# HGRN2 layer on one core: a head's normalised output is kept in z, and its transposes and stores are issued after the next head's projections

## The chip, the cores and the metric

The kernel runs on one NeuronCore of a Trainium2 chip. The metric is the device time of one execution in microseconds; three runs of the kernel before took 3592.83, 3593.45 and 3589.02 us, median 3592.83. The engines of the core are named as in the profile: PE (TensorE, matrix products; PEld is its weight load), DVE (VectorE), ACT (ScalarE), POOL (GpSimd) and SP (SyncE, which only issues transfers here). Each engine works through its own instructions in order, and waits for others by semaphores.

## The reference

Two layers over 1024 latent tokens and 256 context tokens of width 1024. The first runs neighbourhood attention and a bidirectional mLSTM side by side; the second, the one that the change touches, is a bidirectional HGRN2 with 16 heads of key and value width 128. Its essentials (cut):

```python
def project(h):
    q, f_fwd, f_bwd, i, z = _split_cols(h @ w_in, C_SIZES)
    def decay(f_pre):
        f = lb + (1.0 - lb) * jax.nn.sigmoid(f_pre.astype(F32))
        return _bht(_heads(1.0 - f, HG_HEADS)), _bht(_heads(jnp.log(f), HG_HEADS))
    rec = (_bht(_heads(jax.nn.silu(q), HG_HEADS)), _bht(_heads(i, HG_HEADS)), (decay(f_fwd), decay(f_bwd)))
    return rec, z

o_l, o_c = _gla_bidir(rec_l, rec_c, need_ctx)   # gated linear attention, forward plus backward in time

def merge(o, z):
    o = _rms(jnp.swapaxes(o, 1, 2).astype(z.dtype), h_norm.reshape(HG_HEADS, HG_VDIM))
    return (o.reshape(o.shape[:2] + (HG_VW,)) * jax.nn.silu(z)) @ w_out
```

For each head, then: o is computed for all 1024 latent tokens, divided by its root mean square over the 128 channels, scaled per channel by `h_norm`, and multiplied by silu(z). The products of all heads go through `w_out`.

## The kernel before

The kernel is written in a tile framework. The program states operations in a sequence with tiles from pools; a scheduler then orders the instructions on each engine, by priority (the place in the program) and by a time model of its own, and sets the semaphores. A tile of a tag with `bufs` n waits until the tile n places before it in the same tag has been released by all who write or read it.

All large products are made of float32 operands that are split in a high and a low part (`split`, L69 to L72, the high part by ACT, the low one by DVE), in three matmuls for each slab of 128 rows (L117 to L119, and L729 to L731 in the output projection). Their results stand in the PSUM tag `mm`, which has two banks.

The HGRN2 layer runs head by head (L170 to L177), and the scheduler interleaves neighbouring heads:

- `hg_proj` (L756) computes the two decays F (L769, L770) and the query q = silu (L778, L779; `gq`) transposed, with the tokens along the free axis: matmuls of 256 or 512 columns.
- `hg_intra` (L838) and `hg_level` (L884) work out the products within blocks of 128 tokens in seven levels: copies `gksel` by ACT (L893), products by PE (L898), masks and decays by DVE (L905, L907, L918, L920). `hg_near` (L925 to L936) treats neighbours, and `hg_close` (L858) the diagonal; its low part shares the tag `gyt`, one buffer, with the output's eviction.
- `hg_vz` (L782) projects v and z in natural layout, tokens on partitions, two token tiles at a time into one bank of 2 x 256 columns. ACT copies v out (L801), takes the sigmoid of z (L803) and copies z out (L804); POOL multiplies the two in place (L805). The tile z (`gz`) has one buffer for all heads. A first product for the context is copied to `gEc` and transposed (L794).
- `hg_ctx` (L809) makes the states that come out of the context, with scans on DVE (L817, L818) that are started by two memsets (L814, L815).
- `hg_scan` (L938) goes over the eight blocks of 128 tokens. In each, three products (L958, L959, L960) add up in one quarter of the PSUM bank `acc` (one bank); a product of keys and values (L963) and a step on DVE (L965) carry the state on. After four blocks, half a head, the end is worked off:

```python
for i in range(4):
    nc.scalar.activation(jk, o4[:, i, :], AF.Square, accum_out=ss[:, i : i + 1])        # L974, ACT
self.rsqrt(ss, ss, 1.0 / P)                                                             # L142, L144, POOL
pt = self.ps("tr", [P, 4, P])
for i in range(4):
    yn = self.t(pool, [P, P], F32, "gyn", 2)                                            # ring of two
    nc.vector.scalar_tensor_tensor(                                                     # L979, DVE
        out=yn, in0=o4[:, i, :], scalar=ss[:, i : i + 1], in1=z[:, c - 3 + i, :], op0=ALU.mult, op1=ALU.mult)
    nc.tensor.transpose(pt[:, i, :], yn, self.ident)                                    # L982, PE
yt = self.t(pool, [P, 512], F32, "gyt", 1)
nc.scalar.activation(yt, ..., AF.Copy, scale=self.hnc[:, h : h + 1])                    # L984, ACT
nc.gpsimd.dma_start(out=y[h, :, ...], in_=yt)                                           # L985, POOL queue
```

So half a head is four products of 128 x 128 on DVE, four transposes on PE, one eviction of 128 x 512 on ACT and one store to the scratch tensor `yd2` in DRAM.

After the last head, the output projection reads `yd2` back (L716), splits it (`out_y`, L710) and multiplies it by w_out (`out_sum`, L723). For the columns 512 to 1023 it is done in two parts: heads 0 to 7 for all eight token tiles (L1184 to L1187), which the scheduler interleaves with head 15, and then heads 8 to 15 (`out_tile`, L734). The token tiles 0 to 3 need the first half of head 15 from `yd2`, the tiles 4 to 7 the second. SP issues these loads in one queue with the loads of the weights (L97).

Of the kernel before, what the change touches and what calls it, by code (L numbers as in the profile page):

```python
# [9 lines left out]
F32 = mybir.dt.float32  # L10
# [3 lines left out]
ALU = mybir.AluOpType  # L14
# [4 lines left out]
P = 128  # L19
# [24 lines left out]
class Prog:  # L44
# [890 lines left out]
        nc.vector.tensor_tensor(out=pr[1], in0=pr[1], in1=q, op=ALU.mult)  # L935
        H["near"] = pr  # L936

    def hg_scan(self, h, st, halves, S, pool, y):  # L938
        nc = self.nc
        v, z = st["v"], st["z"]  # L940
        Sf, Sb = S
        sb = {7: Sb}
        for c in range(7, 0, -1):
            H = halves[c // 4]
            u = self.ps("s", [P, P])
            nc.tensor.matmul(u, lhsT=H["kn"][1][:, c % 4, :], rhs=v[:, c, :], start=True, stop=True)
            s = self.t(pool, [P, P], F32, "gS1", 10)
            nc.vector.scalar_tensor_tensor(
                out=s, in0=sb[c], scalar=H["T"][:, 1, c % 4 : c % 4 + 1], in1=u, op0=ALU.mult, op1=ALU.add
            )  # L950
            sb[c - 1] = s
        for c in range(8):
            H = halves[c // 4]
            cs = slice((c % 4) * P, (c % 4 + 1) * P)
            if c % 4 == 0:
                o4 = self.ps("acc", [P, 4, P])
            o = o4[:, c % 4, :]
            nc.tensor.matmul(o, lhsT=H["A"][:, c % 4, :], rhs=v[:, c, :], start=True, stop=False)  # L958
            nc.tensor.matmul(o, lhsT=H["Q"][:, 0, cs], rhs=sb[c], start=False, stop=False)  # L959
            nc.tensor.matmul(o, lhsT=H["Q"][:, 1, cs], rhs=Sf, start=False, stop=True)  # L960
            if c < 7:
                u = self.ps("s", [P, P])
                nc.tensor.matmul(u, lhsT=H["kn"][0][:, c % 4, :], rhs=v[:, c, :], start=True, stop=True)  # L963
                s = self.t(pool, [P, P], F32, "gS0", 2)
                nc.vector.scalar_tensor_tensor(  # L965
                    out=s, in0=Sf, scalar=H["T"][:, 0, c % 4 : c % 4 + 1], in1=u, op0=ALU.mult, op1=ALU.add
                )
                Sf = s
            if c % 4 < 3:
                continue  # L970
            ss = self.t(pool, [P, 4], F32, "gss", 2)
            jk = self.t(pool, [P, P], F32, "gjk", 1)
            for i in range(4):
                nc.scalar.activation(jk, o4[:, i, :], AF.Square, accum_out=ss[:, i : i + 1])  # L974
            self.rsqrt(ss, ss, 1.0 / P)
            pt = self.ps("tr", [P, 4, P])
            for i in range(4):
                yn = self.t(pool, [P, P], F32, "gyn", 2)
                nc.vector.scalar_tensor_tensor(  # L979
                    out=yn, in0=o4[:, i, :], scalar=ss[:, i : i + 1], in1=z[:, c - 3 + i, :], op0=ALU.mult, op1=ALU.mult  # L980
                )
                nc.tensor.transpose(pt[:, i, :], yn, self.ident)  # L982
            yt = self.t(pool, [P, 512], F32, "gyt", 1)
            nc.scalar.activation(yt, pt.rearrange("p a b -> p (a b)"), AF.Copy, scale=self.hnc[:, h : h + 1])  # L984
            nc.gpsimd.dma_start(out=y[h, :, (c // 4) * 512 : (c // 4 + 1) * 512], in_=yt)  # L985


    def build(self):
        tc, nc, a = self.tc, self.nc, self.a
        dma = nc.sync.dma_start  # L990
        with ExitStack() as es:
# [19 lines left out]
            def load(name, shape, eng=nc.gpsimd):  # L1011
# [12 lines left out]
                out=self.qkn, in0=qkn[:, 0:1], scalar1=qkn[:, 1:2], scalar2=0.125, op0=ALU.mult, op1=ALU.mult  # L1024
# [14 lines left out]
            for i in range(2):  # L1039
# [6 lines left out]
                out=self.lb[:, 1, :], in0=self.lb[:, 0, :], scalar1=-1.0, scalar2=1.0, op0=ALU.mult, op1=ALU.add  # L1046
# [31 lines left out]
            with tc.tile_pool(name="na", bufs=2) as pool, self.pp.phase(tq=1, s=2, acc=1):  # L1078
                qk = self.na_qk(0, pool)
                z = self.na_z(0, pool)  # L1080
                ahead = [("o", 0), ("z", 0), ("o", 1), ("z", 1), ("o", 2), ("z", 2), ("q", 0), ("k", 0)]
                for p2 in range(8):
# [7 lines left out]
                    if p2 < 7:  # L1090
                        z = self.na_z(p2 + 1, pool)
# [30 lines left out]
            with tc.tile_pool(name="op0", bufs=2) as op, ExitStack() as wl:  # L1122
# [3 lines left out]
                for tt in [8, 9, 3, 4, 2, 5, 1, 6, 0, 7]:  # L1126
# [14 lines left out]
                    out=self.ones, in0=self.ident, scalar1=0.0, scalar2=1.0, op0=ALU.mult, op1=ALU.add  # L1141
# [23 lines left out]
            with l1:  # L1165
                pool = l1.enter_context(tc.tile_pool(name="hg", bufs=2))
                self.rawp = pool
                l1.enter_context(self.pp.phase(s=3, acc=1))
                st = self.hg_proj(0, pool, wf)
                for h in range(16):  # L1170
                    hv = self.hg_intra(st, pool)
                    self.hg_vz(h, st, pool)
                    self.hg_close(hv, pool)
                    S = self.hg_ctx(st, pool)
                    self.hg_scan(h, st, hv, S, pool, self.yd2)
                    if h < 15:
                        st = self.hg_proj(h + 1, pool)

                right.close()
                yp = es.enter_context(tc.tile_pool(name="oy", bufs=1, side="right"))  # L1180
                acc = self.t(yp, [P, 8, 512], F32, "oacc", 1)
                rows = lambda q, b: a["woc"][q * D : (q + 1) * D, b * 512 : (b + 1) * 512]
                w = self.wblock(yp, "wo", [rows(0, 1)], 8, 512, yp, 4, "woraw", ring=8)
                for tt in range(8):  # L1184
                    ps = self.ps("mm", [P, 512])
                    self.out_sum(ps, w, tt, (0,), self.yd2, yp, 2)
                    nc.scalar.copy(acc[:, tt, :], ps)  # L1187
                w2 = self.wblock(yp, "wo", [rows(1, 1)], 8, 512, yp, 4, "woraw", ring=8)
# [152 lines left out]
```

## Time and profile before

| | us |
|---|---|
| median of three runs | 3592.83 |
| lowest, highest | 3589.02, 3593.45 |
| the profiled execution | 3587.84 |
| its span in the profile | 3586.1 |
| PE busy in the span | 3495.6 |
| DVE, ACT, POOL busy | 2235.0, 1456.0, 527.6 |
| mean granted clock of PE (full speed is 1) | 0.992 |

The profile shows one execution. Its page gives busy times by engine, the granted clock in 40 slices, the transfers, and the costliest groups of instructions by source line. Other views of the trace give the waits of one engine (who waited for whom, us in total, times, longest), the busy time by stretch, and the instructions in order of time. In the latter a row has the start, the duration in us, engine, line, operation, the tiles (output <- inputs), shapes and how many were merged; in square brackets stands the idle time of the engine just before, and what ended it. Ends of matmuls are modelled, since they are pipelined: two neighbouring ones overlap, and the distance of their starts says what one costs. In a row of the busy time by stretch stand the stretch, its length, then the busy time and the number of instructions of PE, PEld, DVE, ACT and POOL, the granted clock, the share of the transfer engines' time, and GB/s. The layer takes about 92 us a head, from 1900 to 3450 us of the span.

### The profile page before, as it was taken

What the parts mean: (1) busy time and instruction counts of PE and PEld (TensorE: products, weight loads), DVE (VectorE), ACT (ScalarE), POOL (GpSimd) and SP (SyncE); (2) the same over time, 40 slices, a digit from 0 to 9 for tenths busy, and PEclk for the clock granted to TensorE, in tenths of its full rate; (3) what the DMA queues carried; (4) which work ended last, traced back from release to release, by engine and by line L of the source; (5) the groups of instructions that cost most, each with busy time, mean ns of one, the idle gap of its engine ahead of it and who ended that gap; (6) DMA issues with size and microseconds to landing.
All of it is one profiled execution on the core that took longest, in us unless ns stands there. A gap on an engine that the chain in (4) does not pass through costs nothing.

```text
span 3586.1 us, 64157 instructions
## 1 busy us (share of the span) xinstructions
PE 3495.6 (97%) x24570; PEld 3182.4 (89%) x24570; DVE 2235.0 (62%) x5497; ACT 1456.0 (41%) x3525; POOL 527.6 (15%) x816
## 2 busy tenths in 40 slices
PE   8999999999999999998999999999999999999998
PEld 5879999999999999997788999999999999999877
DVE  4546676666744765664666666666666666666652
ACT  5445555455533333433353333333333333333431
POOL 2222222222211212211010010000000000000100
PEclk9999999999999999999999999999999999999999
DMA  5532222232234434324752111111111111110263
GB/s 211 168 103 76 84 69 84 72 88 76 80 96 145 129 93 139 118 72 140 232 157 60 36 36 33 36 36 36 36 33 36 36 36 33 35 35 22 86 200 108
DMA packets 323043, 305.16 MB, mean 85 GB/s; under 512 B 29016, under 2 KB 280088, under 8 KB 322608
## 3 DMA queue, kind: packets, MB, share of 16 engines
q1 hardware_dynamic: 290704, 217.44, 20.8%
q0 software_dynamic: 32032, 83.61, 6.9%
q8 instruction: 194, 3.18, 0.4%
q14 instruction: 113, 0.93, 0.1%
HBM read 241.49 MB, written 59.30 MB: 84 GB/s over the span
## 4 chain that ended last, share of the span: by engine, by line
PE 49%; issue 5%; DVE 2%; DMA 2%; ACT 2%; POOL 1%; SPq 0%; POOLq 0%; ACTq 0%; DVEq 0%
PE mm L117 10%; PE mm L118 10%; PE mm L119 10%; PE s L898 5%; PE mm L731 2%; PE mm L730 2%; PE mm L729 2%; ACT gjk L974 1%; PE acc L458 1%; DMA wraw<-yd 1%; PE acc L960 1%; PE acc L958 1%; PE acc L959 1%; PE s L467 1%; PE tr L878 1%
## 5 line engine op out<-in xcount | busy, mean ns | idle before, releaser
L119 PE MATMUL mm<-wh,hl 128*128 128x256 f32 x2560 | 748.9, 293 | 0.3 <-DVE hl L250 0.3
L117 PE MATMUL mm<-wh,hh 128*128 128x256 f32 x2560 | 746.6, 292 | 0.3 <-ACT hh L249 0.2
L118 PE MATMUL mm<-wl,hh 128*128 128x256 f32 x2560 | 745.4, 291 | 0.0
L119 PEld LDWEIGHTS mm<-wh,hl 128*128 128x128 f32 x2560 | 488.7, 191 | 11.3 <-issue 4.1
L117 PEld LDWEIGHTS mm<-wh,hh 128*128 128x128 f32 x2560 | 488.6, 191 | 8.4 <-issue 1.4
L118 PEld LDWEIGHTS mm<-wl,hh 128*128 128x128 f32 x2560 | 488.7, 191 | 7.1 <-issue 0.5
L117 PE MATMUL mm<-hh,wh 128*128 128x512 f32 (+1 forms) x1216 | 447.2, 368 | 5.9 <-ACT gFc L769 5.9
L119 PE MATMUL mm<-hh,wl 128*128 128x512 f32 (+1 forms) x1216 | 449.1, 369 | 0.0
L118 PE MATMUL mm<-hl,wh 128*128 128x512 f32 (+1 forms) x1216 | 444.9, 366 | 0.0
L117 PE MATMUL mm<-wzh,hh 128*128 128x256 f32 x1024 | 295.7, 289 | 3.6 <-DVE gq L779 3.6
L118 PE MATMUL mm<-wzl,hh 128*128 128x256 f32 x1024 | 299.1, 292 | 0.0
L119 PE MATMUL mm<-wzh,hl 128*128 128x256 f32 x1024 | 289.1, 282 | 0.0
L117 PEld LDWEIGHTS mm<-hh,wh 128*128 128x128 f32 x1216 | 230.0, 189 | 37.4 <-ACT gFc L769 6.2
L119 PEld LDWEIGHTS mm<-hh,wl 128*128 128x128 f32 x1216 | 229.6, 189 | 34.1
L118 PEld LDWEIGHTS mm<-hl,wh 128*128 128x128 f32 x1216 | 229.7, 189 | 33.9
L729 PE MATMUL mm<-woh,yh 128*128 128x512 f32 x576 | 231.1, 402 | 13.4 <-ACT yh L71 9.2
L71 ACT CAST wh<-wraw 128x512 fp32r<-128x512 f32 x240 | 147.6, 619 | 228.3 <-PE mm L118 157.2
L730 PE MATMUL mm<-wol,yh 128*128 128x512 f32 x576 | 229.7, 399 | 0.4 <-DVE wol L72 0.4
L731 PE MATMUL mm<-woh,yl 128*128 128x512 f32 x576 | 229.4, 399 | 0.4 <-DVE yl L72 0.4
L72 DVE TENSOR_TENSOR wl<-wraw,wh 128x512 fp32r<-128x512 f32 x240 | 164.1, 689 | 91.1 <-ACT wh L71 87.3
L893 ACT COPY gksel<-gK 128x512 f32<-128x512 f32 x192 | 119.7, 632 | 212.1 <-PE s L898 137.0
L898 PE MATMUL s<-gQ,gksel 128*128 128x128 f32 x1536 | 203.7, 277 | 0.1
(318 smaller groups left out, 7536.1 us busy)
## 6 DMA issues: line engine op xcount, KB each, us to landing
wraw<-yd SPq DMA_DIRECT2D x144, 256.0 KB
wraw<-in_wab_dram SPq DMA_DIRECT2D x112, 256.0 KB
md<-ev POOLq DMA_DIRECT2D x100, 256.0 KB, 2.7
wraw<-in_wc_dram SPq DMA_DIRECT2D x96, 256.0 KB
adar<-in_wada_dram POOLq DMA_DIRECT2D x32, 512.0 KB, 4.5
wraw<-in_wc_dram SPq DMA_DIRECT2D x128, 128.0 KB
adar<-in_wada_dram SPq DMA_DIRECT2D x16, 512.0 KB
wraw<-in_wab_dram SPq DMA_DIRECT2D x64, 128.0 KB
```

What stands on the lines that cost most here:

```text
L71: nc.scalar.copy(hi, x)
L72: nc.vector.tensor_tensor(out=lo, in0=x, in1=hi.bitcast(F32), op=ALU.subtract)
L117: mm(ps, lhsT=lh(k), rhs=rh(k), start=(k == 0), stop=False)
L118: mm(ps, lhsT=lh(k), rhs=rl(k), start=False, stop=False)
L119: mm(ps, lhsT=ll(k), rhs=rh(k), start=False, stop=(k == nk - 1))
L458: nc.tensor.matmul(num, lhsT=qc[:, j, :], rhs=C[d][:, j, :], start=False, stop=(j == 1))
L467: nc.tensor.matmul(u, lhsT=st["k"][c][:, j * P : (j + 1) * P], rhs=vw, start=True, stop=True)
L729: mm(ps, lhsT=yh[:, k, :], rhs=w.h(kk), start=(kk == 0), stop=False)
L730: mm(ps, lhsT=yh[:, k, :], rhs=w.l(kk), start=False, stop=False)
L731: mm(ps, lhsT=yl[:, k, :], rhs=w.h(kk), start=False, stop=(kk == 8 * len(qs) - 1))
L893: nc.scalar.copy(ksel.rearrange("p (b s i) -> p b s i", s=2, i=h), pick(K))
L898: nc.tensor.matmul(pa[:, c, :].rearrange("p (b s i) -> p b s i", s=2, i=h), lhsT=ksel[:, c * P : (c + 1) * P], rhs=qp[:, c * nbc : (c + 1) ...
```

## The change

The four products of a half are written into z, in place, instead of a ring of two tiles. The transposes, evictions and stores of both halves go into a function of their own, `hg_out`, which the program calls after the next head's `hg_proj`.

```diff
-    def hg_scan(self, h, st, halves, S, pool, y):
+    def hg_scan(self, st, halves, S, pool):
...
             self.rsqrt(ss, ss, 1.0 / P)
+
+            for i in range(c - 3, c + 1):
+                nc.vector.scalar_tensor_tensor(
+                    out=z[:, i, :], in0=o4[:, i % 4, :], scalar=ss[:, i % 4 : i % 4 + 1], in1=z[:, i, :],
+                    op0=ALU.mult, op1=ALU.mult,
+                )
+
+
+    def hg_out(self, h, yn, pool, y):
+        nc = self.nc
+        for c in range(0, 8, 4):
             pt = self.ps("tr", [P, 4, P])
             for i in range(4):
-                yn = self.t(pool, [P, P], F32, "gyn", 2)
-                nc.vector.scalar_tensor_tensor(
-                    out=yn, in0=o4[:, i, :], scalar=ss[:, i : i + 1], in1=z[:, c - 3 + i, :], op0=ALU.mult, op1=ALU.mult
-                )
-                nc.tensor.transpose(pt[:, i, :], yn, self.ident)
+                nc.tensor.transpose(pt[:, i, :], yn[:, c + i, :], self.ident)
             yt = self.t(pool, [P, 512], F32, "gyt", 1)
             nc.scalar.activation(yt, pt.rearrange("p a b -> p (a b)"), AF.Copy, scale=self.hnc[:, h : h + 1])
-            nc.gpsimd.dma_start(out=y[h, :, (c // 4) * 512 : (c // 4 + 1) * 512], in_=yt)
+            nc.gpsimd.dma_start(out=y[h, :, c * P : (c + 4) * P], in_=yt)
...
                     S = self.hg_ctx(st, pool)
-                    self.hg_scan(h, st, hv, S, pool, self.yd2)
+                    self.hg_scan(st, hv, S, pool)
+                    z = st["z"]
                     if h < 15:
                         st = self.hg_proj(h + 1, pool)
+                    self.hg_out(h, z, pool, self.yd2)
```

The changed file is a few lines longer: there the products stand in L978, the transposes in L989, the evictions in L991 and the stores in L992.

## The prediction

> **What bounds the kernel now.** I read the page's first table, then busy time by stretch, then the waits of TensorE (PE), and last the order of time around the two longest of them.
>
> ```profile
> span 3586.1 us, 64157 instructions
> PE 3495.6 (97%) x24570; PEld 3182.4 (89%) x24570; DVE 2235.0 (62%) x5497; ACT 1456.0 (41%) x3525; POOL 527.6 (15%) x816
> ...
> 3100.00:3200.00 100.00, 98.66 (x670) 90.27 (x669) 65.73 (x127) 37.07 (x84) 8.70 (x10) 1.00 0.13 38
> ...
> PE tr L982 <- DVE gEc L815: 16.0, 15, 1.1
> PE mm L729 <- ACT yh L71: 9.2, 3, 4.8
> PE mm L117 <- DVE gq L779: 3.6, 13, 0.3
> ```
>
> PE is the bound: 97% over the span, 98.66 of 100 us in an undisturbed stretch of the HGRN2 layer. There the change can gain only what PE waits. The list of waits (from 2000 us on) has three large entries: 15 waits of 1.1 us, one for each pair of neighbouring heads, before a transpose of the normalised output (L982); 13 of 0.3 us; and 9.2 us in three waits near the end, the longest 4.8, where the output projection waits for what the last head has stored.
>
> **The wait at L982.** The order of time, PE first, then the engines that feed it (second half of a head):
>
> ```profile
> 3245.52 0.39 PE L960 MATMUL acc<-gS,gQ 128*128 128x128 f32 x2
> ...
> 3250.06 0.31 PE L982 MATMUL tr<-ident,gyn 128*128 128x128 f32 x1
> 3250.21 0.38 PE L794 MATMUL tr<-ident,gEc 128*128 128x128 f32 x2
> 3250.43 0.27 PE L982 MATMUL tr<-ident,gyn 128*128 128x128 f32 x1
> 3251.77 0.33 PE L982 MATMUL tr<-ident,gyn 128*128 128x128 f32 x1 [1.07 <-DVE gEc L815]
> ...
> 3248.26 1.34 POOL L144 TENSOR_TENSOR gss<-gss,mhalf 128x4 f32<-128x4 f32 x1
> 3249.64 0.61 DVE L979 SCALAR_TENSOR_TENSOR gyn<-acc,gss,gz 128x128 f32<-128x128 f32 x2 [0.32 <-POOL gss L144]
> 3250.16 0.68 DVE L935 TENSOR_TENSOR gkn<-gkn,gq 128x512 f32<-128x512 f32 x1
> 3250.76 0.69 DVE L918 TENSOR_TENSOR gK<-gK,gF 128x512 f32<-128x512 f32 x1
> 3251.37 0.35 DVE L979 SCALAR_TENSOR_TENSOR gyn<-acc,gss,gz 128x128 f32<-128x128 f32 x1
> ```
>
> The ring gyn has two buffers. Products one and two fill it; product three needs the first buffer back, which PE frees at 3250.37, but DVE has by then taken up L935 and L918, so product three comes at 3251.37 and transpose three at 3251.77. The releaser named, L815, is only the DVE instruction that the profile saw last. The cost by starts: 1.34 us between two transposes that need 0.11 (the two of L794 take 0.22), so 1.23 us, more than the 1.07 of idle time, since ends on PE are modelled.
>
> **The change, part by part.** No instruction is added or removed: 128 products, 128 transposes, 32 evictions and 32 stores stay, with the same shapes. What goes is the ring; what moves is where the scheduler puts things. I compared the instruction order of the built programs, engine by engine; up to the first HGRN2 head it is the same.
>
> (1) The products (now L978) stand on DVE as four in a row. In the second half they stand ahead of L918, L935, L918, as only two did before. On PE, behind the last product pair of the second half, there stand 56 projection matmuls of 256 columns before the first transpose. These cost 0.12 each:
>
> ```profile
> 3233.72 0.28 PE L118 MATMUL mm<-hl,wzh 128*128 128x256 f32 x1
> 3233.84 0.28 PE L119 MATMUL mm<-hh,wzl 128*128 128x256 f32 x1
> 3234.40 0.38 PE L117 MATMUL mm<-wzh,hh 128*128 128x256 f32 x1 [0.28 <-DVE gq L779]
> ...
> 3229.32 0.40 PE L118 MATMUL mm<-hl,wh 128*128 128x512 f32 x1
> 3229.55 0.39 PE L960 MATMUL acc<-gS,gQ 128*128 128x128 f32 x2
> 3229.77 0.39 PE L963 MATMUL s<-gv,gkn 128*128 128x128 f32 x2
> ...
> 3232.52 1.53 POOL L144 TENSOR_TENSOR gss<-gss,mhalf 128x4 f32<-128x4 f32 x1
> ```
>
> So, told on the clock of this head, PE comes to the first transpose 0.22 + 56 x 0.12 = 6.9 us after the pair at 3245.52 (a scan pair takes 0.22, 3229.55 to 3229.77), at 3252.4. The products start when POOL is done, at 3249.6; two take 0.52 (3249.64 to 3250.16), four 1.1: ready at 3250.8, with 1.6 us to spare. In the first half two scan pairs, 11 matmuls of 512 columns (0.23, 3229.32 to 3229.55) and 24 of 256 stand behind the last product pair at 3229.55: 0.22 + 0.45 + 2.5 + 2.9 = 6.1, so 3235.6. POOL ends at 3234.05, and four products later it is 3235.2. Slack 0.4. From head 0 to head 1 the order is tighter (fewer matmuls stand between the last transpose and the next tile), so I count half of that wait. Term: 14.5 x 1.23 = -17.8 us; bounds 0 and -18.5.
>
> The four products do add a wait on DVE: they reach the queue's head some 0.9 us before POOL is done, since L918 no longer runs first. Behind them stand L918, L935, L918 and the next head's scans L817, L818; ACT's level copies (L893) wait for these, and PE's level products (L898) for the copies. DVE works 65.73 of 100 us, and PE has 20 projection matmuls (2.4 us) between the last transpose and the first of those products: cost nothing. Without that cover it would be 0.9 a head. The eviction (L991, ACT) and the store (L992, POOL) keep their neighbours in both queues: the first half's store stands before the second half's inverse root, the second's before the first product of z and its sigmoid (L805). On SP only the end moves: the reload of head 15's first half stands behind one weight load instead of seven. That is worth nothing, since SP had issued these before the store landed.
>
> (2) The wait at L117 for gq (L779): 0.56 from start to start instead of 0.12, so 0.44, 13 times, 5.7 us. L779 now comes behind four products, L918, L72, L935, L918 (0.6 each): 3234.8 + 2.4 + 0.7 = 3237.9. PE gets there after three transposes, eight scan pairs at 0.22 and one transpose: 3235.6 + 0.34 + 1.8 + 0.11 = 3237.85. A wait of about 0.1 is left; I take -3 us, bounds -5.7 and +2 (POOL 0.5 us later in each head).
>
> (3) The end, where head 15's halves are stored and read back for the output projection:
>
> ```profile
> 3425.63 0.38 PE L982 MATMUL tr<-ident,gyn 128*128 128x128 f32 x2
> 3427.24 0.68 ACT L984 ACTIVATE gyt<-tr,hnc 128x512 f32<-128x512 f32 x1
> ...
> 3428.22 4.99 DMA yd<-gyt
> 3434.19 4.44 DMA wraw<-yd
> ...
> 3431.74 0.39 PE L960 MATMUL acc<-gS,gQ 128*128 128x128 f32 x2
> 3436.96 0.80 PE L729 MATMUL mm<-woh,yh 128*128 128x512 f32 x1 [4.83 <-ACT yh L71]
> 3438.40 0.63 PE L729 MATMUL mm<-woh,yh 128*128 128x512 f32 x1
> 3438.83 0.63 PE L730 MATMUL mm<-wol,yh 128*128 128x512 f32 x1
> ...
> 3451.29 0.38 PE L982 MATMUL tr<-ident,gyn 128*128 128x128 f32 x2
> 3461.06 0.39 PE L731 MATMUL mm<-woh,yl 128*128 128x512 f32 x1
> 3465.32 0.80 PE L729 MATMUL mm<-woh,yh 128*128 128x512 f32 x1 [3.87 <-ACT yh L71]
> 3468.48 0.39 PE L731 MATMUL mm<-woh,yl 128*128 128x512 f32 x1
> ...
> 3366.00:3372.00 6.00, 2.94 (x16) 1.74 (x14) 5.48 (x10) 5.90 (x13) 0.00 (x0) 1.00 1.01 308
> 3372.00:3377.00 5.00, 4.91 (x15) 3.68 (x14) 5.00 (x10) 4.21 (x8) 0.00 (x0) 0.66 0.84 260
> ```
>
> The two waits cost 5.0 and 4.0 by starts (5.2 and 4.3, less one step), and behind each the matmuls come at 0.43 instead of 0.23, half the clock, for some ten and eight of them: 1.9 and 1.5 us more. Together 12.4. The chain from the last transpose to the resumed matmul is 11.1 us (3425.9 to 3436.96), 1.3 of it before L984, in which ACT is busy with weight casts. In the changed order PE has 38 matmuls and four scan pairs, 38 x 0.23 + 0.9 = 9.6 us, before it needs that data, and ACT no casts ahead: about 1.0 of the 5.0 is left. The second half's transposes came in two pairs, the later 14.3 us after PE resumed; now all four come some 5 us after, so the store goes 9 us earlier and covers the 4.0. Against it stands a new wait: on ACT one of the second half's squares comes behind a cast that waits for weights, and POOL, the products and the transposes behind that; I put it at 1 us, as an estimate from the 1.3. Term: 12.4 - 2.0 = -10.4; bounds 0 and -12.4.
>
> Whether a small rest of waits costs clock is open. In 3366 to 3372 PE works 2.94 of 6 us, in three separate waits, and the clock of the next 5 us is 0.66. The Trainium skill, "TensorE: Matmul & The Clock Gate", Part 1, has half clock after an idle window of about 3.4 us. By that, the rests above are free; by the row, short waits close together also cost, up to 1.9 us here. I go by the row and leave it in the range.
>
> Sum: -17.8 - 3 - 10.4 = -31.2 us. Against the profiled execution, 3587.84 with its 1.7 us around the span, that is 3556.6; the median of the runs, 3592.83, lies 5.0 higher, so **3562 us**.
>
> **Rivals.** (A) Slower: z has one buffer, and its release now hangs on PE's transposes instead of DVE's products. The next head's copies into z (L804, ACT) wait for them, and those free the bank in which PE starts the next tile but one.
>
> ```profile
> 3252.21 2.12 PE L898 MATMUL s<-gQ,gksel 128*128 128x128 f32 x16
> 3252.58 0.37 ACT L804 COPY gz<-mm 128x256 f32<-128x256 f32 x1
> 3252.85 0.69 ACT L984 ACTIVATE gyt<-tr,hnc 128x512 f32<-128x512 f32 x1
> ```
>
> Between the last transpose and that tile the new order has 20 matmuls and two groups of L898 (the 16 records above): 2.4 + 1.9 = 4.3 us; needed are eviction and copy, 1.1 us and a hop. It decides only if ACT, held by copies that wait for DVE, is over 3 us late, and makes the kernel slower from 31 / 15 = 2.1 us a head beyond that; at 3.2 us, 15 x 3.2 = 48 less 31, it gives about 3610. The row of ACT (37.07 of 100 busy) speaks against. The Trainium skill, "Trainium Kernel Development and Optimization", Best Practices, asks for double buffers; taken alone that rule is for this rival. (B) The wait stays: the transposes meet products as late as before, because DVE, not the ring, was late. Then only (3) is gained: 3582. L935 and L918, 1.2 us between the pairs, speak against. (C) The end gains nothing, since store and reload (4.99 and 4.44) are DMA latency: 3562 + 10.4 = 3572. (D) It doesn't do what it says: in the new order the transposes stand among the next head's v and z projections, as they did, some 20 matmuls later, and not behind all its projections. For this speaks that order; if what the ring cost is lost again at another wait, 3590. Against it: nothing in the order stands closer behind its source than before, apart from (2).
>
> **Chances.** Forecast 0.57 (its own range 3554 to 3570), C 0.16, B 0.12, D 0.07, A 0.08. Faster by over 0.2% (7.2 us, about what a measurement can tell): 0.57 + 0.16 + 0.12 = 0.85; within 0.07; slower 0.08. The range, 3554 to 3588, takes in C and B.
>
> **What would show it.** The waits of PE from 2000 us on have no 15 waits before the transposes (now L989); L117 on L779 under 3 us in total; a stretch of 100 us with PE above 99; in the last 150 us no wait over 2 us before L729. Wrong would be: a PE wait before L117 released by ACT L804 (A), 15 waits at L989 (B), 4 us at L729 (C).

## The result, and the profile after

The changed kernel takes 3550.84 us (median of four runs, 3547.99 to 3552.64), against 3592.89 for the kernel before on the same chip: a ratio of 0.9884, 95% interval 0.9867 to 0.9902. That is faster, as forecast, but by 42 us instead of 31, and 3 us under the low end of the range. Its profiled execution took 3550.99 us.

The page of the changed kernel, span and busy time; then its busy time by stretch (stretch, length, busy time of PE, PEld, DVE, ACT, POOL with instructions, granted clock, share of the transfers, GB/s):

```profile
span 3549.2 us, 64265 instructions
PE 3485.2 (98%) x24570; PEld 3181.6 (90%) x24570; DVE 2239.0 (63%) x5497; ACT 1454.8 (41%) x3525; POOL 525.2 (15%) x816
```

```profile
3100.00:3200.00 100.00, 100.00 (x684) 92.17 (x683) 67.21 (x134) 33.12 (x77) 8.90 (x10) 1.00 0.12 36
```

The instruction counts of all five engines are those of before. In the undisturbed stretch PE is busy for 100.00 of 100 us, where it was 98.66. Now the whole list of what PE waited for from 2000 us on (who for whom: us in total, times, longest):

```profile
PE mm L731 <- DVE yl L72: 1.6, 1, 1.6
PE tr L878 <- ACT gkn L880: 1.4, 1, 1.4
PE mm L729 <- ACT yh L71: 1.3, 2, 1.1
PE s L868 <- ACT gsg L71: 1.1, 1, 1.1
PE mm L729 <- ACT woh L71: 1.1, 1, 1.1
PE mm L729 <- DVE oacc L743: 0.7, 1, 0.7
PE mm L117 <- ACT gz L804: 0.4, 1, 0.4
```

All three large entries of before are gone: no transpose of a normalised output (now L989) waits, L779 is not on the list, and of the waits of 4.8 and 3.9 us for head 15's stored halves neither is left. The 1.1 us at L729 for `yh` stand at 3341.64, before the new kernel has stored anything of head 15 (its first half is stored at 3394.25): that is the first matmul of the output projection, which had waited 0.5 us in the kernel before too. Rival A's mechanism (L804) appears once, with 0.4 us.

Where the gain lies can be read from one line of code. L831 runs in one place of each head (8 of its 128 matmuls), so its first and last starts frame the heads, and the rest of the span is the end. Before, then after:

```profile
L831 PE MATMUL s<-gv,gknc x128: 270/275/275, 2007.7 to 3387.2; 128*128 128x128 f32 x128
```

```profile
L831 PE MATMUL s<-gv,gknc x128: 270/275/275, 2007.5 to 3357.4; 128*128 128x128 f32 x128
```

From first to last it was 1379.5 us and is 1349.9: the heads gain 29.6. From the last to the end of the span it was 3586.1 - 3387.2 = 198.9 and is 191.8: the end gains 7.1. The period of a head in between is 92.13 us before and 90.03 after.

In the order of time of the second half of a head (POOL, DVE, then PE), the four products are one row of 1.13 us, and PE comes to them with time to spare:

```profile
3216.13 1.65 POOL L144 TENSOR_TENSOR gss<-gss,mhalf 128x4 f32<-128x4 f32 x1
...
3217.81 1.13 DVE L978 SCALAR_TENSOR_TENSOR gz<-acc,gss,gz 128x128 f32<-128x128 f32 x4 [0.33 <-POOL gss L144]
3218.85 0.69 DVE L918 TENSOR_TENSOR gQ<-gQ,gF 128x512 f32<-128x512 f32 x1
...
3220.24 0.27 PE L989 MATMUL tr<-ident,gz 128*128 128x128 f32 x1
3220.57 0.27 PE L989 MATMUL tr<-ident,gz 128*128 128x128 f32 x1
3220.80 0.28 PE L989 MATMUL tr<-ident,gz 128*128 128x128 f32 x1
3221.16 0.27 PE L989 MATMUL tr<-ident,gz 128*128 128x128 f32 x1
```

The products are done at 3218.9, the first transpose starts at 3220.24: 1.3 us to spare (1.6 were forecast). The wait of DVE for POOL that the prediction announced, some 0.9 us, is 0.33 here, and was 0.32 at this place before. Over 2100 to 3300 us such waits rose from 4.1 us in 13 to 12.7 us in 26, so what is new is mostly the first half's. They cost PE nothing.

### The profile page after: what moved, and what is told of

Its sections match the earlier page's. It is cut to its first block, busy times and chain, and to the rows that moved or that the text cites. A ratio compares the mean times of both kernels' runs of the same rounds, so it can differ in the third digit from the quotient of the medians.

```text
span 3549.2 us, 64265 instructions
## 1 busy us (share of the span) xinstructions
PE 3485.2 (98%) x24570; PEld 3181.6 (90%) x24570; DVE 2239.0 (63%) x5497; ACT 1454.8 (41%) x3525; POOL 525.2 (15%) x816
## 4 chain that ended last, share of the span: by engine, by line
PE 85%; issue 6%; DMA 4%; DVE 2%; ACT 1%; POOL 1%; SPq 0%; POOLq 0%; DVEq 0%; ACTq 0%
PE mm L119 18%; PE mm L117 18%; PE mm L118 18%; PE s L898 5%; PE acc L674 2%; PE mm L729 2%; PE mm L731 2%; PE mm L730 2%; PE tr L654 2%; PE acc L458 2%; PE s L467 2%; DMA mld<-md 1%; PE acc L448 1%; PE acc L958 1%; PE acc L959 1%
## 5 line engine op out<-in xcount | busy, mean ns | idle before, releaser
L117 PE MATMUL mm<-wh,hh 128*128 128x256 f32 x2560 | 746.4, 292 | 0.1
L118 PE MATMUL mm<-wl,hh 128*128 128x256 f32 x2560 | 745.4, 291 | 0.0
L117 PEld LDWEIGHTS mm<-wh,hh 128*128 128x128 f32 x2560 | 488.6, 191 | 8.0 <-issue 1.4
L118 PEld LDWEIGHTS mm<-wl,hh 128*128 128x128 f32 x2560 | 488.6, 191 | 7.1 <-issue 0.5
L117 PE MATMUL mm<-hh,wh 128*128 128x512 f32 (+1 forms) x1216 | 447.0, 368 | 5.9 <-ACT gFc L769 5.9
L118 PE MATMUL mm<-hl,wh 128*128 128x512 f32 (+1 forms) x1216 | 450.5, 371 | 0.0
L117 PE MATMUL mm<-wzh,hh 128*128 128x256 f32 x1024 | 299.2, 292 | 0.4 <-ACT gz L804 0.4
L118 PE MATMUL mm<-wzl,hh 128*128 128x256 f32 x1024 | 291.4, 285 | 0.0
L117 PEld LDWEIGHTS mm<-hh,wh 128*128 128x128 f32 x1216 | 230.0, 189 | 40.4 <-ACT gFc L769 6.2
L118 PEld LDWEIGHTS mm<-hl,wh 128*128 128x128 f32 x1216 | 230.2, 189 | 32.2
L729 PE MATMUL mm<-woh,yh 128*128 128x512 f32 x576 | 230.4, 400 | 7.5 <-ACT woh L71 3.9
L72 DVE TENSOR_TENSOR wl<-wraw,wh 128x512 fp32r<-128x512 f32 x240 | 163.8, 688 | 93.6 <-ACT wh L71 85.0
L898 PE MATMUL s<-gQ,gksel 128*128 128x128 f32 x1536 | 204.2, 276 | 0.0
```

The costliest lines, as they stand in the source:

```text
L72: nc.vector.tensor_tensor(out=lo, in0=x, in1=hi.bitcast(F32), op=ALU.subtract)
L117: mm(ps, lhsT=lh(k), rhs=rh(k), start=(k == 0), stop=False)
L118: mm(ps, lhsT=lh(k), rhs=rl(k), start=False, stop=False)
L729: mm(ps, lhsT=yh[:, k, :], rhs=w.h(kk), start=(kk == 0), stop=False)
L898: nc.tensor.matmul(pa[:, c, :].rearrange("p (b s i) -> p b s i", s=2, i=h), lhsT=ksel[:, c * P : (c + 1) * P], rhs=qp[:, c * nbc : (c + 1) ...
```

## The experiments

Eight runs were made, each with its own profile. In the table, heads and end are read as above from the first and last start of L831 and the span of each profile. The column "lost in the end" is worked out from the trace: over 60 to 120 us behind the last projection matmul, the distance from each PE start to the next, less what that instruction takes undisturbed (0.2275 us for an output matmul, 0.112 for 128 columns), summed. The ratio is that to runs of the kernel before on the same chip.

| kernel | head period | heads | end | lost in the end | median | ratio (interval) |
|---|---|---|---|---|---|---|
| before | 92.13 | 1379.5 | 198.9 | 12.6 | 3588.66 to 3592.89, by chip | 1 |
| changed | 90.03 | 1349.9 | 191.8 | 5.1 | 3550.84 | 0.9884 (0.9867 to 0.9902) |
| e1_ring4 | 90.55 | 1355.9 | 187.0 | 0.9 | 3551.49 | 0.9895 (0.9881 to 0.9908) |
| e2_z_only | 90.03 | 1349.7 | 194.1 | 7.3 | 3554.13 | 0.9902 (0.9889 to 0.9916) |
| e3_last_head | 92.13 | 1380.3 | 189.8 | 3.6 | 3578.48 | 0.9967 (0.9955 to 0.9979) |
| e4_ring3 | 91.57 | 1372.8 | 201.1 | 14.8 | 3581.08 | one run |
| e5_after_again | 90.03 | 1350.8 | 190.6 | 4.0 | 3552.14 | 0.9893 (0.9879 to 0.9908) |
| e6_late_out | 90.55 | 1354.3 | 198.1 | 11.8 | 3561.66 | 0.9921 (0.9906 to 0.9935) |
| e7_last_late | 90.03 | 1349.7 | 198.7 | 12.0 | 3558.92 | 0.9913 (0.9896 to 0.993) |
| e8_ring1 | 101.5 | 1513.9 | 203.5 | 17.1 | 3725.88 | one run |

### Was it the ring? Four buffers

```diff
-            s = self.t(pool, [P, P], F32, f"gS{d}", 10 if d else 2)
+            s = self.t(pool, [P, P], F32, f"gS{d}", 8 if d else 2)
...
-            s = self.t(pool, [P, P], F32, "gS1", 10)
+            s = self.t(pool, [P, P], F32, "gS1", 8)
...
-                yn = self.t(pool, [P, P], F32, "gyn", 2)
+                yn = self.t(pool, [P, P], F32, "gyn", 4)
```

> The kernel before with a ring gyn of four buffers in place of two (the ring gS1 gives up two of its ten for the room); neither is z reused nor is anything moved. If the ring alone made the wait at the third transpose, the head period falls from 92.13 to 90.0 +- 0.3 us and nearly the whole gain is there: 3546 to 3558 us, ratio 0.988 to 0.990, no wait before L982 among PE's waits. If the place of the output stage behind the next head's projections is what counts, the period stays above 91.2 us and the time above 3575.

With the ring gS1 cut to eight and gyn left at two, the instruction order of the built program is that of before, so the cut by itself changes nothing. The waits of PE in the kernel with four buffers, then the second half of a head on DVE and PE:

```profile
PE mm L117 <- DVE gq L779: 3.5, 13, 0.3
PE tr L878 <- ACT gkn L880: 1.4, 1, 1.4
PE s L868 <- ACT gsg L71: 1.1, 1, 1.1
PE mm L729 <- ACT yh L71: 0.2, 1, 0.2
```

```profile
3222.24 1.13 DVE L979 SCALAR_TENSOR_TENSOR gyn<-acc,gss,gz 128x128 f32<-128x128 f32 x4 [0.32 <-POOL gss L144]
3223.28 0.68 DVE L935 TENSOR_TENSOR gkn<-gkn,gq 128x512 f32<-128x512 f32 x1
...
3224.69 0.27 PE L982 MATMUL tr<-ident,gyn 128*128 128x128 f32 x1
```

The wait at L982 is gone without z and without the move, and so is the time: the median is that of the changed kernel within its scatter. The ring was the cause. The period missed its expectation of 90.0 +- 0.3: it is 90.55, and the 0.52 us that are missing have a name in the list, the 13 waits at L117, which stayed as they were before. In their place the end is better by 4.8 us than in the changed kernel, so the sums are nearly equal. That they come out equal is luck; what the ring explains is the 23.6 us of the heads and the end without the two long waits.

### Is the move worth anything? z in place, stage where it was

```diff
-                yn = self.t(pool, [P, P], F32, "gyn", 2)
+                yn = z[:, c - 3 + i, :]
```

> The products go into z, as in the change, but the transposes, evictions and stores stay in the source where they were, inside the scan of each half. If the move is worth nothing, this equals the changed kernel: 3551 +- 7 us, head period 90.0 +- 0.2. If the move is worth part of the gain, the head period stays above 90.6 and the time above 3560.

The heads are equal to a hundredth (90.03). The call behind the next projections is worth nothing there: the scheduler had put both versions' transposes at the same places but for one (the fourth of the first half stands eight pairs of scan products later in the changed kernel); in the second half both have 56 projection matmuls between the last scan product and the first transpose. The only difference is in the end, 2.3 us for the changed kernel, and the intervals of the two ratios overlap. The move with the ring of two kept was not run.

### The end by itself

```diff
-                    self.hg_scan(h, st, hv, S, pool, self.yd2)
                     if h < 15:
+                        self.hg_scan(h, st, hv, S, pool, self.yd2)
                         st = self.hg_proj(h + 1, pool)
+                    else:
+                        self.hg_scan_z(st, hv, S, pool)
+                        self.hg_out(h, st["z"], pool, self.yd2)
```

(`hg_scan_z` is the `hg_scan` of the changed kernel.)

> Heads 0 to 14 as before, only head 15 as in the change. This leaves the term of the end alone. By the two traces it is 6.8 us: 3586 +- 2 us, ratio 0.998. By the predicted term it is 10.4: 3582.5. If the end gained only because it was entered at another phase from changed heads, it is 3593, ratio 1.000.

The four largest waits of PE:

```profile
PE tr L982 <- DVE gEc L815: 16.0, 15, 1.1
PE mm L117 <- DVE gq L779: 3.5, 13, 0.3
PE s L868 <- ACT gsg L71: 1.4, 1, 1.4
PE mm L729 <- ACT yh L71: 1.2, 2, 1.0
```

The heads keep their waits and their period, and the long waits at L729 are gone. From the first L831 on, 1379.5 + 198.9 - 1380.3 - 189.8 = 8.3 us are gained; by the runs it is 3588.66 - 3578.48 = 10.2, with an interval from 7.5 to 16. So the end's term exists without the heads. The profile puts it between the two sizes expected, 6.8 and 10.4; the medians put it at the predicted one, with 6.8 outside the interval. The time is under both figures expected, which had started from 3592.8 for the kernel before.

### One buffer more, one buffer less

The first edit is e4 (with gS1 at eight, as in e1), the second e8 (with gS1 at ten):

```diff
-                yn = self.t(pool, [P, P], F32, "gyn", 2)
+                yn = self.t(pool, [P, P], F32, "gyn", 3)
...
-                yn = self.t(pool, [P, P], F32, "gyn", 2)
+                yn = self.t(pool, [P, P], F32, "gyn", 1)
```

> Ring gyn of three (gS1 of eight), else as before. Ring theory: the third product no longer waits, the fourth still comes behind the two level products (1.2 us); PE reaches it 7 matmuls later than before, so a wait of about 0.5 us a head stays in place of 1.40: head period 91.0 to 91.5, about 3578 us. If the ring were not the cause, the period stays at 92.1; if the first step away from two buffers were enough, it is 90.0.

> The kernel before with a ring gyn of one buffer: every product waits for the transpose ahead of it. Ring theory: the head period rises above 92.13, by an estimate from the series (ring 4 90.55, ring 3 91.57, ring 2 92.13) to between 92.5 and 94.5, and the time to 3595 to 3625. If the scheduler finds other work for PE between the transposes, which it can since they now stand 16 to 32 matmuls apart, the period is 92.1 or less.

A ring of three: first the wait, then the heads.

```profile
PE tr L982 <- DVE gyn L979: 7.0, 15, 1.1
```

```profile
L831 PE MATMUL s<-gv,gknc x128: 270/275/275, 2005.4 to 3378.2; 128*128 128x128 f32 x128
```

7.0 / 15 = 0.47 us a head are left, as expected, yet the period is 91.57, 1.02 more than with four buffers, instead of at most 91.5. The matmuls behind the wait lose time as well: in the single records the steps from the transpose before the wait on are 0.68, 0.44 and 0.22 us, where 0.11, 0.12 and 0.12 are usual, together 0.99 more. The named releaser is now the product itself, L979, which confirms how the L815 of before was read. A ring of one:

```profile
PE tr L982 <- DVE gyn L979: 75.5, 31, 4.1
```

```profile
3164.61 0.39 PE L960 MATMUL acc<-gS,gQ 128*128 128x128 f32 x2
3169.12 0.48 PE L982 MATMUL tr<-ident,gyn 128*128 128x128 f32 x1 [4.12 <-DVE gyn L979]
```

```profile
3000.00:3100.00 100.00, 93.80 (x620) 86.01 (x619) 60.37 (x119) 31.65 (x75) 9.41 (x10) 0.95 0.10 31
```

Here my estimate missed by far: the period varies from 98.9 to 101.9 with a median of 101.5, not 92.5 to 94.5. The series of four, three, two, one buffers is 90.55, 91.57, 92.13, 101.5. With one buffer every product needs a round trip from PE to DVE, with other work of DVE in between. The two waits in each head, of 4.1 and of 0.6 to 0.9 us, are both in the second half, and the longer one is not such a round trip: the first half's transposes now stand among the projection matmuls that came later before, so that in the second half the first transpose follows the last scan product with no other matmul in between (above), and PE waits for all that leads to the first product. These waits are 75.5 us where they were 16.0, so 4.0 of the 1513.9 - 1379.5 = 134.4 us, or 9.0 a head, that the heads are longer than before. The rest was not taken apart; part of it is clock, which is 0.95 in the stretch shown and was 1.00 before.

### Holding z longer

```diff
+                    p = self.tc.cur_priority
+                    self.tc.cur_priority = p + 1000000
                     self.hg_out(h, z, pool, self.yd2)
+                    self.tc.cur_priority = p
```

> The changed kernel with the output stage at the lowest priority of the scheduler: all eight transposes of a head then stand on PE behind 50 projection matmuls after the last scan product, and z is held longer. Rival A (z held): 15 waits of PE before L117 released by ACT L804, head period 90.3 to 92, time above 3555. If z is free early enough even so, the period stays 90.0 and no such waits are listed. For the end, head 15's first half is stored only with its second half: if the store of the first half is what PE waited for in the kernel before, the waits at L729 come back (over 3 us in the last 150).

Products of the first half and the eight transposes of that head, on DVE and PE; then the three largest waits of PE:

```profile
3212.65 1.11 DVE L978 SCALAR_TENSOR_TENSOR gz<-acc,gss,gz 128x128 f32<-128x128 f32 x4
...
3227.43 1.03 PE L989 MATMUL tr<-ident,gz 128*128 128x128 f32 x8
```

```profile
PE mm L729 <- ACT yh L71: 6.0, 3, 4.4
PE mm L117 <- DVE gq L779: 3.3, 12, 0.3
PE tr L989 <- DVE gz L978: 1.7, 1, 1.7
```

The first half's transposes come 14.8 us behind its products, and still PE waits nowhere for L804. That presses rival A only a little, since the second half's transposes, which come last in both kernels, set when z is free: the first copy into z comes 6.7 us behind the sigmoid (L803) of the same bank, where it is 5.0 in the changed kernel. With these 1.7 us more rival A has no force. The period rises to 90.55 all the same, since the 12 waits at L117 are back: without the transposes in front, PE reaches that tile too early again. And with the first half stored late, the wait at L729 is back, 4.4 us.

### Storing only head 15 late

```diff
+                    p = self.tc.cur_priority
+                    if h == 15:
+                        self.tc.cur_priority = p + 1000000
                     self.hg_out(h, z, pool, self.yd2)
+                    self.tc.cur_priority = p
```

> The changed kernel with only head 15's output stage at low priority: the first transpose stands 4 projection matmuls later, the other seven 19 output matmuls behind the last scan product in place of 32. The heads stay at 90.03. If the order of weight casts and reloads around the stores sets what PE still loses after the last projection (15.0 us over its matmuls in the changed kernel, 10.1 in the ring of four), this moves by 2 us or more either way: below 3549 or above 3553; if only the time of the store counts, the first half's store is some 8 us later and it is 3555 or more.

Stores on POOL and the waiting matmul:

```profile
3405.94 0.60 POOL L992 DMA_DIRECT2D yd<-gyt  x1
3409.80 0.55 POOL L992 DMA_DIRECT2D yd<-gyt  x1 [3.26 <-ACT gyt L991]
...
3412.26 0.80 PE L729 MATMUL mm<-woh,yh 128*128 128x512 f32 x1 [4.73 <-ACT yh L71]
```

In the changed kernel the same store was issued here:

```profile
3394.25 0.61 POOL L992 DMA_DIRECT2D yd<-gyt  x1 [8.04 <-ACT gyt L991]
```

Counted from the last projection (3333.46 here, 3332.22 there), the first half's store is 72.5 instead of 62.0 us behind it, and the matmul that waits is the 205th of the output projection, the same as the one that waited 4.83 us in the kernel before. Heads unchanged, the end 6.9 us worse, and 6.8 us more in the medians of this chip. So the time of that store does set this wait, as the second expectation had it.

### The changed kernel again

No edit.

> The changed kernel once more, unedited, beside more runs of the kernel before. If the 5 us by which the first median of before lay over its profiled execution were scatter of the stage ahead of the HGRN2 heads, the ratio is that of the spans (36.9 of 3586.1): 0.9897, with before near 3588.5 and this near 3551.5. If before really lies at 3593, the ratio stays at 0.988.

0.9893, with before at 3590.27 (seven runs) and the changed kernel at 3552.14. Over all 21 runs the kernel before lies between 3587.20 and 3594.51 with a median of 3589.34, not 3593. The interval holds both ratios; the medians speak for the first expectation. The 21 runs come from more than one chip (median 3592.89 beside the result, 3588.66 beside e1 to e4, 3590.27 here), so scatter and chip are not told apart.

## Why the prediction came out as it did

**What failed.** Two steps of the sum: term (1) priced a wait at the ring at 1.23 us, and it cost 1.57, so that the term came out at -23.6, beyond its bound of -18.5; and 5.0 us were added to the profiled time, although nothing in the change bore on them; the changed kernel's median, 3550.84, does not lie above its profiled time, 3550.99. The first made 5.8 of the 11.2 us between 3562 and 3550.84, the second 5.0; terms (2) and (3), 3.0 too small and 3.3 too large, cancelled, which is luck. Mechanism and direction held: every sign that the prediction named for itself came, and of those against it only one wait of 0.4 us (A).

**The direction and the cause were right.** The ring of two made the wait at L982; e1 shows it by changing the ring alone. That the transposes go among the next head's v and z projections, not behind all its projections, was right too: e2 gets the same heads without the move. In that sense rival D holds for half of the change: the move does nothing that can be measured. A wait that is the same in each of 15 heads, on the engine that should never wait, is what the Trainium skill, "Perfetto Trace Analysis", Optimization Strategy, reads as a possible lack of buffers; e1 agrees, with 1.58 us a head for two buffers more.

**Term (1), -17.8, was too small: -23.6** (e1: 1379.5 - 1355.9). I priced one step, from the second to the third transpose, 1.23 us. But the fourth product comes 0.26 us behind the third on DVE, and the fourth transpose cannot follow in 0.11. The trace of before has the two transposes as one row, and the level products behind them:

```profile
3251.77 0.61 PE L982 MATMUL tr<-ident,gyn 128*128 128x128 f32 x2 [1.07 <-DVE gEc L815]
3252.21 0.99 PE L898 MATMUL s<-gQ,gksel 128*128 128x128 f32 x6
```

From 3251.77 to 3252.21 two transposes took 0.44 instead of 0.22 (0.28 and 0.17 in the single records, so 0.17 and 0.06 more), and the first step of L898 was 0.22 instead of 0.12 there. Added up, 1.23 + 0.17 + 0.06 + 0.11 = 1.57 us a head, all of which e1 gave back (1.58). The step that failed is "so 1.23 us": it stopped at the resumed instruction.

**Term (2), -3, was too small: -6.0** (the gain of the changed kernel's heads less that of e1's, 29.6 - 23.6). Nothing of the wait is left, where I had kept 0.1 in each head, and behind each of the 13 waits one more step was 0.11 longer, so that it cost 0.55 and not 0.44. That is 7.1 us in all; the intervals of the first and last heads take back the rest. The mechanism was the one described, L779 comes later and PE later still, but that the margin came out near nil was luck. The forecast has the four products done at 3235.2 and then starts the four instructions ahead of L779 at 3234.8; from 3235.2 L779 would end at 3238.3, 0.45 us after PE, and the wait would have stayed. It went because the first transpose came 0.9 us behind the products (3206.47 to 3207.41) and not 0.4.

```profile
3207.41 0.49 PE L989 MATMUL tr<-ident,gz 128*128 128x128 f32 x3
...
3208.79 0.68 DVE L779 TENSOR_TENSOR gq<-gsg,mm 128x512 f32<-128x512 f32 x1
...
3209.55 0.37 PE L117 MATMUL mm<-wzh,hh 128*128 128x256 f32 x1
```

L779 ends at 3209.47, and PE arrives at 3209.55. That the margin is 0.1 us is why e1 and e6, which have these transposes and scan products behind that tile and not in front of it, have the wait again.

**Term (3), -10.4, was too large: -7.1.** The two waits that I priced are gone with the slow matmuls behind them: all of the 12.6 us, where I had left 1.0 of the first. But PE lost 5.1 us at other places, where I had put 1:

```profile
3405.74 0.50 PE L729 MATMUL mm<-woh,yh 128*128 128x512 f32 x1 [1.11 <-ACT woh L71]
...
3419.87 0.47 PE L729 MATMUL mm<-woh,yh 128*128 128x512 f32 x1 [0.66 <-DVE oacc L743]
...
3422.18 0.50 PE L731 MATMUL mm<-woh,yl 128*128 128x512 f32 x1 [1.61 <-DVE yl L72]
```

The first waits for a weight cast. The other two begin the fourth token tile: the profile names the sum on DVE that reads a result bank (L743), then the low part of a tile of heads 8 to 11 (L72). Around the first, transfers are busy 0.97 of the time:

```profile
3400.00:3410.00 10.00, 8.70 (x38) 6.15 (x37) 5.85 (x11) 5.15 (x11) 2.05 (x3) 1.00 0.97 292
```

That the share of 0.97 is their cause was not tried by itself. What the table shows is that the loss in the end goes from 0.9 (e1) to 17.1 (e8) among kernels that run the same matmuls there in another order. The range for this term, 0 to -12.4, held it; its middle could not be had from one trace.

**The offset, +5.0, was the other error.** I added the distance of the profiled execution from the median of three runs, as if the profile had been lucky. Two of the three runs were high: the median of 21 is 3589.34, 1.5 above the profile. Where the scatter comes from stays open. L831 starts for the first time between 2003.9 and 2008.7 us in the ten profiles, but the profile of before, a short run, is with 2007.7 among the late ones, and the two profiles of the changed kernel differ by 0.8 us ahead of the heads, 0.9 in them and 1.2 in the end. Measured from profile to profile the gain is 23.6 + 6.0 + 7.1 = 36.7 and 0.2 ahead of the heads, which is the difference of the two spans, 36.9. The 42 us of the first comparison are that and the height of the runs of before. My 31.2 from the profile would have been 3556.6; these 36.7 with the 5.0 added would have been 3556.1.

**The rivals.** A: once 0.4 us, and not with the copy into z 1.7 us later (e6). B: out, L935 and L918 did stand between the products because of the ring. C: out, by e3 alone. Of the clock I had left open what short waits close together do. In the changed kernel they cost again at the start of the output projection, where PE waits 1.4, 1.1 and 1.1 us:

```profile
3338.00:3344.00 6.00, 3.68 (x10) 2.02 (x11) 4.62 (x9) 4.69 (x10) 0.00 (x0) 0.60 0.96 298
```

but not in the stretch from 3400 to 3410, with 1.1 and 0.2 us (clock 1.00, above). The Trainium skill, "TensorE: Matmul & The Clock Gate", Part 1, names an idle window of about 3.4 us; no single wait here is that long, and the clock still fell to 0.60. Why the one stretch lost clock and the other did not, no run here separates.

## What to carry to other kernels

When an engine in strict order waits for the third item of four, look at the depth of the ring between it and the producer before looking at where the code stands: two more buffers did what a reorganised loop did, and moving the call added nothing that could be measured. Price a wait up to the first instruction that runs at its usual distance again, not up to the resumed one. And where a median of three runs and a profile differ by as much as the runs scatter, don't add the difference to a forecast.

## What the runs showed of the hardware

Behind a wait of PE, one step soon after the resumed matmul is about twice as long: 0.22 for 0.12 at L898 behind each of the 15 waits at L982 in the kernel before, and 0.22 for 0.12 at L118 behind each of its 13 waits at L117. Why is not shown. These 0.11 us are in no list of waits; the two together are a tenth of the 2.1 us that a head gained. The idle time that the list names for the wait at L982, 1.07 us, was two thirds of what it cost, 1.57. With waits of 1.1 and 0.3 us in each head the granted clock stayed at 1.00 (before, 3100 to 3200 us); with one of 4.1 us in each head it was 0.95 (e8, 3000 to 3100 us).
